# Two product-key expert layers on one core: softmax, transposes, small transfers and GpSimd's table emitted a slot or more after their input, and row gathers issued in every slot

## The chip, the cores and the metric

The kernel runs on one core of one Trainium2 chip. A core has TensorE (PE) for matrix products, with its weight loads shown apart (PEld), VectorE (DVE), ScalarE (ACT), GpSimd (POOL) and SyncE (SP), each with a queue of its own that it works off in order, and 16 DMA engines. The metric is the device time of one execution in microseconds (us).

## The reference, cut to what matters

Two blocks run one after the other on 256 tokens of width 1024. The first (four sequence mixers and an MLP) is not touched. The second adds 16 meta tokens (272 in all) and has two layers, each a mixer (pooling in layer 0, stick-breaking attention in layer 1) followed by a PEER layer: for every token 8 heads pick 16 of 16,384 experts each, and the token gets the sum of the picked experts' outputs.

```
s = einsum('bthpc,hpnc->bthpn', q, sub_keys)            # 8 heads, 2 halves, 128 sub-keys
top_s, top_i = lax.top_k(s, 16)                         # per half
cand_s = (top_s[..., 0, :, None] + top_s[..., 1, None, :])   # 256 candidates
cand_i = (top_i[..., 0, :, None] * 128 + top_i[..., 1, None, :])
best_s, best_pos = lax.top_k(cand_s, 16)
expert = take_along_axis(cand_i, best_pos)
gate = softmax(best_s)
act = gelu(einsum('btd,bthkd->bthk', hx, u[expert]))
y = einsum('bthk,bthkd->btd', gate * act, v[expert])
```

All of it is in fp32.

## The kernel before, in words

A PEER layer is `peer(l, ...)`, called for l = 0 and 1 (272 and 256 tokens). It does not gather the picked experts for most tokens. For 224 "dense" tokens it computes all 16,384 activations, multiplies them by a gate that is zero where the expert was not picked, and multiplies by all of v. The remaining 48 tokens (32 in layer 1) are "sparse": for each group of 16 of them 32 gathers bring the picked rows of u and then of v, one row in each of 128 partitions (512 KB per gather), and a DVE instruction, called a step here, multiplies or accumulates each.

Weights come in chunks of 128 x 1024 (512 KB). `_Stream` loads each into a raw buffer by SP's queue, ACT copies it rounded into a hi buffer (L256), and DVE or POOL subtracts the two into a lo buffer (L267; which one is said by `ULO` and `VLO`; in the U pass POOL takes the first 32 chunks and then three of each four). A projection (`proj`) is then 24 matmuls: 16 with hi and 8 with lo.

The **U pass** of a layer has 128 slots, `c` = 0 to 127, one u chunk in each. In the hand-made order of a slot come: `activate(c - 1)`, ACT's gelu of the chunk before (and, for tokens whose gates have already been made, DVE's product); `gates_out`, which takes finished gates out of PSUM; the hi and lo splits of a later chunk; sparse gathers and steps; ACT's `scaled` work for gates; DVE's routing work; the projection; gate matmuls. The first chunks do not need gates: a value waits in `row(c)` for them.

Routing work is the generator `routing()`: `route(8, ...)` for tokens 0 to 127 and then for the other dense and some of the sparse ones, in layer 0 also `topk_c` and `route(1, ...)` for the rest; then 56 groups of `onehots(j)`, one for each four dense tokens. A group's one-hot tiles oAB (compared with the index) and oHL (scaled by the gate, on DVE for every third group, on ACT for the others) feed 8 gate matmuls (`gates(j)`). There are three sets of these tiles. Each piece of routing says what it costs DVE, and a slot takes pieces until its budget `SLOT` is used up; yielding "slot" ends the slot's routing work, yielding a function runs it on PE after the slot's projection. When 128 slots are over and groups are left, the loop goes on with slots that have no projection.

Inside `route`: DVE adds the pairs of half scores (`pairs` after the change), POOL adds the pairs of indices into a table (L1006, L1009), `top16` finds the best 16 per head on DVE, ACT takes the exponent, DVE divides, PE transposes indices and gates to columns (`to_cols`). `finish_full(1)` sends the sparse tokens' indices and gates through DRAM by four small transfers on ACT's queue (L1069, L1070). Gathers (`fetch`, L1240) are issued on POOL's queue into two buffers in the U pass; `EARLY` says from which slot, `RS` how many steps a slot gets (0.4 and 0.2), and `held` are the buffers issued and not used.

The **V pass** has 128 chunks and two more gather buffers, `RV` steps per chunk. Most instructions carry line L200, the helper that records every operation.

Of the kernel before, what the change touches and what calls it, by code (L numbers as in the profile page):

```python
# [13 lines left out]
U32 = mybir.dt.uint32  # L14
# [5 lines left out]
P = 128  # L20
# [13 lines left out]
SLOT = 2800  # L34
# [254 lines left out]
def _build(nc, tc, A, O):  # L289
    pool_cm = tc.tile_pool(name="s", bufs=1)  # L290
    ps_cm = tc.tile_pool(name="ps", bufs=1, space=PSUM)
    with pool_cm as pool, ps_cm as pp:
# [604 lines left out]
        def peer(l, n, h, mixer, outer, qh, ql, end):  # L897
# [40 lines left out]
            best, pos, posf, ee, gg, dd, sm = (R(1) for _ in range(7))  # L938

# [27 lines left out]
            def top16(src, tv, iv):  # L967
                V.max(tv[0], src)
                V.max_index(iv[0].bitcast(U32), tv[0], src)
                V.match_replace(src, tv[0], src, -3.0e38)  # L970
                yield (600, 0, 0)
                V.max(tv[1], src)
                V.max_index(iv[1].bitcast(U32), tv[1], src)
                yield (400, 0, 0)
# [8 lines left out]
            def route(nh, tp, ix, finish):  # L983
# [12 lines left out]
                for eng, dst, s1, s2 in ((V, cand, v3(tp[:, 0]), v3(tp[:, 1])), (G, cex, v3(idxf[:, 0]), v3(idxf[:, 1]))):  # L996
# [14 lines left out]
                    yield ((1000, 0, 0) if eng is V else (0, 0, 1700))  # L1011
                for hd in range(nh):
                    yield from top16(cand[:, hd], halves(best[:, 0], 16 * hd), halves(pos[:, 0], 16 * hd))
                V.tensor_copy(posf[:, 0, 0:w], pos[:, 0, 0:w].bitcast(U32))
                V.tensor_sub(v3(dd[:, 0]), v3(best[:, 0]), v3(best[:, 0])[:, :, 0:1].broadcast_to([P, nh, 16]))
                S.activation(gg[:, 0, 0:w], dd[:, 0, 0:w], AF.Exp)
# [22 lines left out]
            def to_cols(e_src, g_src, a, b):  # L1039
# [6 lines left out]

                yield both
# [12 lines left out]
            def finish_full(j):  # L1060
                def g():
                    yield from to_cols(ee[:, 0, :], gg[:, 0, :], P * j, min(P * j + P, nd))
                    yield (1200, 0, 0)
                    if j:
                        a, m = nd - P, (SEQ - nd) // 16
                        pi = pos[:, 0].bitcast(U32)
                        V.tensor_copy(pi, ee[:, 0])
                        for dr, dst, src in ((sp_dr[0], sp_e, pi), (sp_dr[1], sp_g, gg[:, 0])):
                            nc.scalar.dma_start(dr[0:m].rearrange("g (t h) k -> (g t) (h k)", h=8), src[a:P])  # L1069
                            nc.scalar.dma_start(dst[:, 0:m], dr[0:m].rearrange("g p k -> p g k"))  # L1070
                        yield (150, 0, 0)
                return g
# [6 lines left out]
            def topk_c():  # L1079
                for hf in range(2):  # L1080
                    yield from top16(fold[:, hf], halves(topc[:, 0], 16 * hf), halves(idxc[:, 0], 16 * hf))
# [76 lines left out]
            scale_q, ready, mm, out_q = [], {}, [0], []  # L1158
# [84 lines left out]
            def gather():  # L1243
                q = mode["q"]
                if q == -1:
                    fetch(srow, sp_rows, row16[:, 0:1])
                elif q < len(js) and free:
                    g, j = js[q]
                    held.append(free.pop(0))
                    fetch(held[-1], A[f"ur{l}" if j < 16 else f"v{l}"], sp_e[:, g, j % 16:j % 16 + 1])  # L1250
                else:
                    return
# [16 lines left out]
            def sparse():  # L1269
                for i, (g, j) in enumerate(js):  # L1270
                    gather()
                    gather()
                    b, k = held.pop(0), j % 16
# [49 lines left out]
            with tc.manual_schedule():  # L1323
                c = 0
                while c < P or work is not None or scale_q or mm[0] < nq or out_q:
# [18 lines left out]
                    if c >= EARLY[l] and c >= mode["rdy"] and c < P:  # L1344
                        if c % 3 == 0 and mode["q"] < 4:
                            gather()
                        if mode["q"] > 0 and mode["n"] < 31:
                            bal_d -= 1300 * steps(RS[l])
# [25 lines left out]
                if c == P:  # L1374
                    activate(P - 1)

# [346 lines left out]
```

## Time and profile before

| | us |
|---|---|
| median of 3 runs (2188.49 to 2190.12) | 2190.11 |
| profiled execution, own time | 2184.81 |
| its span | 2182.8 |
| PE busy | 2062.6 (94%) |
| DVE busy | 1605.4 (74%) |
| ACT busy | 1271.5 (58%) |
| POOL busy | 1097.8 (50%) |
| mean granted TensorE clock | 0.966 of full speed |

In the span, layer 0's U pass runs from 418 to 862 us and its V pass from 870 to 1207; layer 1's from 1451 to 1844 and from 1852 to the end. Busy shares are means over stages; a stretch's own row says what holds it. A row of the timeline reads: start, duration, engine, line, operation, tiles out<-in, shapes, count, and in brackets how long the engine had stood idle before and what ended that.

### The profile page before, as it was taken

To read this page: it belongs to the slowest core of one execution; us is meant where nothing else is said; L and a number is where in the kernel's file an instruction comes from. 1 tells how busy PE (TensorE), PEld (TensorE's weight loads), DVE (VectorE), ACT (ScalarE), POOL (GpSimd) and SP (SyncE) were. 2 spreads that over 40 slices of the span, in tenths; PEclk is the share of its full clock that TensorE was granted. 3 is DMA by queue.
4 is the path that set the end of the run, shared out by engine and by line. 5 is a ranking of instruction groups with operands and counts; after the bars stand their busy time and mean duration, and the time that the engine had idled before them with its cause. 6 is when DMAs were issued, how large, how long until landed. Compare 5 with 4: busy or idle time off the path is not lost. (4 is left out here: it accounts for less than half of the span.)

```text
span 2182.8 us, 42173 instructions
## 1 busy us (share of the span) xinstructions
PE 2062.6 (94%) x15924; PEld 1981.2 (91%) x15924; DVE 1605.4 (74%) x3187; ACT 1271.5 (58%) x2572; POOL 1097.8 (50%) x671
## 2 busy tenths in 40 slices
PE   8889999888998888999999999988999999999999
PEld 6789998888998887999999988888999998999998
DVE  7964846998566567788887575699757766878875
ACT  4654444554876766555554665445688886555554
POOL 5746736576676656233332351457677766233210
PEclk8999999999999999999999997999999999999999
DMA  5336662354565656899997420534566667888874
GB/s 183 135 117 203 205 188 95 118 158 158 184 215 200 206 194 229 315 332 341 313 318 251 153 87 20 175 121 156 172 212 207 211 215 244 309 312 322 304 254 145
DMA packets 127964, 451.55 MB, mean 207 GB/s; under 512 B 16577, under 2 KB 19777, under 8 KB 126993
## 3 DMA queue, kind: packets, MB, share of 16 engines
q1 hardware_dynamic: 100192, 352.86, 49.0%
q0 software_dynamic: 24592, 88.32, 10.9%
q10 hardware_dynamic: 2976, 7.68, 1.0%
q8 instruction: 126, 2.06, 0.4%
q14 instruction: 78, 0.63, 0.1%
HBM read 445.00 MB, written 3.67 MB: 206 GB/s over the span
## 5 line engine op out<-in xcount | busy, mean ns | idle before, releaser
L200 PE MATMUL bank<-XX,hi 128*128 128x224 f32 (+3 forms) x7360 | 1152.9, 306 | 30.8 <-ACT hi L256 18.3
L200 PEld LDWEIGHTS bank<-XX,hi 128*128 128x128 f32 x7360 | 1017.9, 195 | 63.2 <-ACT hi L256 21.1
L267 POOL TENSOR_TENSOR lo<-raw,hi 128x1024 fp32r<-128x1024 f32 x276 | 674.6, 2456 | 448.8 <-ACT hi L256 398.9
L256 ACT ACTIVATE hi<-raw 128x1024 fp32r<-128x1024 f32 x616 | 650.2, 1057 | 410.3 <-PE bank L200 374.9
L200 PE MATMUL bank<-XX,lo 128*128 128x224 f32 (+2 forms) x4672 | 637.1, 278 | 20.8 <-POOL lo L267 14.2
L200 PEld LDWEIGHTS bank<-XX,lo 128*128 128x128 f32 x4672 | 601.4, 193 | 31.9 <-POOL lo L267 17.7
L267 DVE TENSOR_TENSOR lo<-raw,hi 128x1024 fp32r<-128x1024 f32 x340 | 434.5, 1278 | 168.0 <-ACT hi L256 143.7
L200 ACT ACTIVATE big<-bank 128x256 f32<-128x256 f32 (+45 forms) x400 | 126.3, 321 | 150.1 <-DVE big L200 95.8
L200 DVE TENSOR_TENSOR big<-big,bank 128x256 f32<-128x256 f32 (+41 forms) x313 | 94.4, 302 | 145.2 <-ACT big L200 135.8
L200 ACT ACTIVATE oHL<-oAB,picks 128x128 f16<-128x128 f16 x592 | 189.2, 391 | 19.1 <-DVE oAB L200 19.1
L200 DVE SCALAR_TENSOR_TENSOR big<-big 128x1024 f32<-128x1024 f32 (+5 forms) x89 | 109.2, 1232 | 42.1 <-DMA big<-ur,sp_e 32.3
L1240 POOL DMA_INDIRECT big<-ur,sp_e x56 | 80.3, 1434 | 89.2 <-DVE big L200 84.2
L1240 POOL DMA_INDIRECT big<-v,sp_e x47 | 70.6, 1501 | 107.9 <-DVE big L200 105.5
L200 DVE TENSOR_TENSOR oAB<-bank,picks 128x1024 f16<-128x1024 f32 (+1 forms) x112 | 114.0, 1035 | 0.0
L200 PE MATMUL bank<-big 128*128 128x128 f32 (+9 forms) x472 | 87.7, 314 | 11.6 <-ACT big L200 9.0
L200 ACT ACTIVATE XX<-big 128x224 fp32r<-128x224 f32 (+1 forms) x216 | 81.6, 378 | 28.4 <-DVE big L200 28.2
L200 ACT ACTIVATE big<-big 128x416 f32<-128x416 f32 (+5 forms) x120 | 53.9, 469 | 65.0 <-DVE big L200 58.8
L200 PE MATMUL bank<-oHL,oAB 128*128 128x128 f16 x896 | 68.7, 223 | 23.5 <-DVE oHL L200 13.9
L200 PEld LDWEIGHTS bank<-big 128*128 128x128 f32 (+3 forms) x472 | 66.8, 195 | 24.4 <-ACT big L200 11.3
L200 DVE TENSOR_TENSOR XX<-big,XX 128x224 fp32r<-128x224 f32 (+1 forms) x214 | 86.2, 404 | 0.0
L256 ACT ACTIVATE hi<-more 128x1024 fp32r<-128x1024 f32 x48 | 50.9, 1061 | 57.2 <-PE bank L200 55.2
L200 PEld LDWEIGHTS <-oAB 128*128 128x128 f16 x896 | 52.6, 99 | 27.5 <-issue 25.3
(189 smaller groups left out, 2389.7 us busy)
## 6 DMA issues: line engine op xcount, KB each, us to landing
raw<-u SPq DMA_DIRECT2D x256, 512.0 KB
raw<-v SPq DMA_DIRECT2D x208, 512.0 KB
raw<-w SPq DMA_DIRECT2D x64, 512.0 KB
more<-v SPq DMA_DIRECT2D x48, 512.0 KB
raw<-wq SPq DMA_DIRECT2D x32, 512.0 KB
raw<-win SPq DMA_DIRECT2D x16, 512.0 KB
raw<-wkv SPq DMA_DIRECT2D x16, 512.0 KB
raw<-wout SPq DMA_DIRECT2D x8, 512.0 KB
```

Of the source, the lines that this page charges most:

```text
L200: i = f(*a, **k)
L256: nc.scalar.activation(hi, raw, AF.Copy)
L267: eng.tensor_sub(self.lo[i % self.nh], raw, self.hi[i % self.nh].bitcast(F32))
L1240: nc.gpsimd.indirect_dma_start(out=dst, out_offset=None, in_=src, in_offset=bass.IndirectOffsetOnAxis(ap=at, axis=0))
```

## The change

It touches the order in which `peer` emits its work, and four numbers that the planner goes by. In `route`, POOL's table of index pairs is emitted with the fourth head's `top16` (or the last, where there are fewer) instead of right after DVE's pairs; a new "slot" stands ahead of ACT's exponent, and one ahead of the transposes. The planner's costs of `top16` go from 600 and 400 to 1000 and 550 in `route` and to 1150 and 750 in `topk_c`, and `SLOT` from 2800 to 2700. The sparse tokens' indices and gates are copied to rows of their own, and their transfers are put off: out two slots later, back five slots later. In the U pass a gather is issued in each slot in which a buffer is free, once those transfers are out, and a step is made only when the oldest gather is three slots old. In the V pass every free buffer is filled ahead of a step.

```
-SLOT = 2800
+SLOT = 2700
+            pout, gout = R(1)[:, 0], R(1)[:, 0]
-            def top16(src, tv, iv):
+            def top16(src, tv, iv, cost=(600, 400)):
-                yield (600, 0, 0)
+                yield (cost[0], 0, 0)
-                yield (400, 0, 0)
+                yield (cost[1], 0, 0)
-                for eng, dst, s1, s2 in ((V, cand, v3(tp[:, 0]), v3(tp[:, 1])), (G, cex, v3(idxf[:, 0]), v3(idxf[:, 1]))):
+                def pairs(eng, dst, s1, s2):
-                    yield ((1000, 0, 0) if eng is V else (0, 0, 1700))
+                pairs(V, cand, v3(tp[:, 0]), v3(tp[:, 1]))
+                yield (1000, 0, 0)
                 for hd in range(nh):
-                    yield from top16(cand[:, hd], halves(best[:, 0], 16 * hd), halves(pos[:, 0], 16 * hd))
+                    if hd == min(nh - 1, 3):
+                        pairs(G, cex, v3(idxf[:, 0]), v3(idxf[:, 1]))
+                    yield from top16(cand[:, hd], halves(best[:, 0], 16 * hd), halves(pos[:, 0], 16 * hd), (1000, 550))
+                yield "slot"
                 S.activation(gg[:, 0, 0:w], dd[:, 0, 0:w], AF.Exp)
                 yield "slot"
...
+                yield "slot"
                 yield both
...
-                        pi = pos[:, 0].bitcast(U32)
+                        pi = pout.bitcast(U32)
                         V.tensor_copy(pi, ee[:, 0])
-                        for dr, dst, src in ((sp_dr[0], sp_e, pi), (sp_dr[1], sp_g, gg[:, 0])):
-                            nc.scalar.dma_start(dr[0:m].rearrange("g (t h) k -> (g t) (h k)", h=8), src[a:P])
-                            nc.scalar.dma_start(dst[:, 0:m], dr[0:m].rearrange("g p k -> p g k"))
-                        yield (150, 0, 0)
+                        V.tensor_copy(gout, gg[:, 0])
+                        def there():
+                            for dr, src in ((sp_dr[0], pi), (sp_dr[1], gout)):
+                                nc.scalar.dma_start(dr[0:m].rearrange("g (t h) k -> (g t) (h k)", h=8), src[a:P])
+                        def back():
+                            for dr, dst in ((sp_dr[0], sp_e), (sp_dr[1], sp_g)):
+                                nc.scalar.dma_start(dst[:, 0:m], dr[0:m].rearrange("g p k -> p g k"))
+                        later.append((state["c"] + 2, there))
+                        later.append((state["c"] + 5, back))
+                        yield (300, 0, 0)
...
-                    yield from top16(fold[:, hf], halves(topc[:, 0], 16 * hf), halves(idxc[:, 0], 16 * hf))
+                    yield from top16(fold[:, hf], halves(topc[:, 0], 16 * hf), halves(idxc[:, 0], 16 * hf), (1150, 750))
...
-                    held.append(free.pop(0))
+                    held.append((free.pop(0), state["c"]))
...
-                    gather()
-                    gather()
-                    b, k = held.pop(0), j % 16
+                    while not held or (state["c"] >= P and free and mode["q"] < len(js)):
+                        gather()
+                    (b, _), k = held.pop(0), j % 16
...
-                    if c >= EARLY[l] and c >= mode["rdy"] and c < P:
-                        if c % 3 == 0 and mode["q"] < 4:
-                            gather()
-                        if mode["q"] > 0 and mode["n"] < 31:
-                            bal_d -= 1300 * steps(RS[l])
+                    while later and later[0][0] <= c:
+                        later.pop(0)[1]()
+                    if c >= EARLY[l] and c >= mode["rdy"] and c < P and not later:
+                        gather()
+                        mode["c"] = min(mode["c"] + RS[l], 1.5)
+                        if held and held[0][1] <= c - 3 and mode["n"] < 31:
+                            bal_d -= 1300 * steps(0)
...
+                state["c"] = P
+                mode["c"] = 0.0
```

The first place is POOL's queue at layer 0's first table, before and then after. `lo`, `raw` and `hi` are the buffers of u chunks; the rows of L1006 and L1009 (L1008 and L1011 in the changed kernel) are the table.

```order
L1101 DMA big<-big 16x2x128
L1006 TENSOR_TENSOR big<-big 128x8x16
L1006 TENSOR_TENSOR big<-big 128x8x8
L1006 TENSOR_TENSOR big<-big 128x8x5
L1006 TENSOR_TENSOR big<-big 128x8x4
L1006 TENSOR_TENSOR big<-big 128x8x3
L1009 TENSOR_TENSOR big<-big 128x8x2 x3
L1006 TENSOR_TENSOR big<-big 128x8x8
L267 TENSOR_TENSOR lo_76<-raw_72,hi_73 128x1024
L267 TENSOR_TENSOR lo_77<-raw_69,hi_74 128x1024
```

```order
L1118 DMA big<-big 16x2x128
L267 TENSOR_TENSOR lo_76<-raw_72,hi_73 128x1024
L267 TENSOR_TENSOR lo_77<-raw_69,hi_74 128x1024
L1008 TENSOR_TENSOR big<-big 128x8x16
L1008 TENSOR_TENSOR big<-big 128x8x8
L1008 TENSOR_TENSOR big<-big 128x8x5
L1008 TENSOR_TENSOR big<-big 128x8x4
L1008 TENSOR_TENSOR big<-big 128x8x3
L1011 TENSOR_TENSOR big<-big 128x8x2 x3
L1008 TENSOR_TENSOR big<-big 128x8x8
L267 TENSOR_TENSOR lo_78<-raw_70,hi_75 128x1024
```

The two lo splits that stood behind the table now stand ahead of it.

The second place is ACT's queue at layer 0's small transfers. The rows to `lo_4244<-bank` or `big<-bank` are gelus of whole chunks, `sp` is the DRAM buffer, `sp_e` and `sp_g` the sparse tokens' indices and gates.

```order
L256 ACTIVATE hi_73<-raw_71 128x1024
L1069 DMA sp<-big 32x128
L1070 DMA sp_e<-sp 128x2x16
L1069 DMA sp<-big 32x128
L1070 DMA sp_g<-sp 128x2x16
L200 ACTIVATE lo_4244<-bank_68 128x224
L256 ACTIVATE hi_74<-raw_72 128x1024
```

```order
L1080 DMA sp<-big 32x128 x2
L200 ACTIVATE big<-bank_62 128x224
L256 ACTIVATE hi_73<-raw_71 128x1024
L200 ACTIVATE big<-bank_68 128x224
L256 ACTIVATE hi_74<-raw_72 128x1024
L200 ACT_TABLE_LOAD
L200 ACTIVATE big<-big 128x16
L200 ACT_TABLE_LOAD
L200 ACTIVATE big<-bank_63 128x224
L256 ACTIVATE hi_75<-raw_69 128x1024
L1084 DMA sp_e<-sp 128x2x16
L1084 DMA sp_g<-sp 128x2x16
```

Both transfers out now go together, and those back stand three gelus and hi copies behind them, with the exponent of `route(1)` between.

The third place is ACT's queue at the end of layer 0's U pass. `bank<-bank` and `big<-bank` are the gelu of a chunk's gated and of its other tokens, `oHL` rows the scalings of a gate group (8 make one group), `WW` the first operands of the V pass.

```order
L200 ACTIVATE oHL_1_4252<-oAB_1_4249,picks 128x128 x4
L200 ACTIVATE bank_62<-bank_62 128x220
L200 ACTIVATE big<-bank_62 128x4
L256 ACTIVATE hi_73<-raw_70 128x1024
L200 ACTIVATE bank_68<-bank_68 128x220
L200 ACTIVATE big<-bank_68 128x4
L200 ACTIVATE WW_0_9402<-lo_4244 128x224
L200 ACTIVATE WW_1_9403<-lo_4244 128x224
```

```order
L200 ACTIVATE bank_68<-bank_68 128x188
L200 ACTIVATE big<-bank_68 128x36
L200 ACTIVATE oHL_2_4253<-oAB_2_4250,picks 128x128 x4
L200 ACTIVATE oHL_1_4252<-oAB_1_4249,picks 128x128 x8
L200 ACTIVATE oHL_2_4253<-oAB_2_4250,picks 128x128 x8
L200 ACTIVATE oHL_1_4252<-oAB_1_4249,picks 128x128 x8
L200 ACTIVATE oHL_2_4253<-oAB_2_4250,picks 128x128 x8
L200 ACTIVATE oHL_1_4252<-oAB_1_4249,picks 128x128 x8
L200 ACTIVATE WW_0_9375<-lo_4244 128x224
L200 ACTIVATE WW_1_9376<-lo_4244 128x224
```

When the last chunk's gelu runs, 188 tokens have their gates instead of 220, and the scalings of five groups and a half stand between it and the V pass.

## Rows read from the trace of the kernel before

**Rows 1.** Busy time by stretch: stretch, its length, then each engine's busy us.

```profile
core 0: us, PE busy (x) PEld busy (x) DVE busy (x) ACT busy (x) POOL busy (x), PEclk, DMA share, GB/s
418.40:541.20 122.80, 104.22 (x866) 102.43 (x865) 108.87 (x354) 56.12 (x87) 85.82 (x62) 0.94 0.48 153
...
618.50:861.80 243.30, 211.15 (x1896) 205.13 (x1897) 162.86 (x268) 164.16 (x452) 155.32 (x78) 0.96 0.61 200
...
869.80:1207.00 337.20, 335.42 (x2133) 319.73 (x2133) 274.51 (x382) 176.16 (x269) 110.68 (x70) 0.99 0.88 309
1451.30:1558.20 106.90, 93.75 (x768) 92.66 (x766) 97.60 (x333) 45.77 (x71) 73.37 (x47) 0.92 0.47 150
1558.20:1844.20 286.00, 285.09 (x2746) 283.70 (x2746) 195.32 (x353) 239.30 (x642) 204.29 (x91) 1.00 0.63 209
```

**Rows 2.** Timeline of PE, two projections' starts in layer 1's late U pass.

```profile
1710.34 1.95 PE L200 MATMUL bank<-XX,hi 128*128 128x224 f32 x16
...
1713.02 1.95 PE L200 MATMUL bank<-XX,hi 128*128 128x224 f32 x16
```

**Rows 3.** Work on the tiles oHL by stretch: PE (gate matmuls), DVE, ACT.

```profile
618.50:861.80 243.30, 26.26 (x312) 15.82 (x13) 67.56 (x212) 0.96 0.61 200
...
1558.20:1844.20 286.00, 31.18 (x440) 21.92 (x18) 94.52 (x296) 1.00 0.63 209
```

**Rows 4.** Waits of PE, 1558.2 to 1844.2: us, times, longest.

```profile
PE bank L200 <- POOL lo L267: 0.8, 2, 0.4
```

**Rows 5.** Timeline of POOL at the first table of layer 0, then of layer 1.

```profile
426.47 1.77 POOL L1006 TENSOR_TENSOR big<-big 128x128 f32<-128x128 f32 x5 [3.75 <-DVE big L200]
...
429.03 6.99 POOL L267 TENSOR_TENSOR lo<-raw,hi 128x1024 fp32r<-128x1024 f32 x3
...
1461.81 1.86 POOL L1006 TENSOR_TENSOR big<-big 128x128 f32<-128x128 f32 x5 [7.52 <-DVE big L200]
```

**Rows 6.** Timeline of ACT: layer 0's second exponent, layer 1 after the small transfers.

```profile
483.26 0.31 ACT L200 ACTIVATE big<-big 128x128 f32<-128x128 f32 x1 [6.11 <-DVE big L200]
...
1556.88 0.36 ACT L200 ACTIVATE lo<-bank 128x224 f32<-128x224 f32 x1 [9.57 <-DMA sp<-big]
```

**Rows 7.** Waits of DVE, 618.5 to 861.8: us, times, longest.

```profile
DVE big L200 <- DMA big<-ur,sp_e: 27.2, 7, 6.6
DVE big L200 <- DMA big<-v,sp_e: 16.4, 4, 5.7
```

**Rows 8.** DVE's instructions by form, 600 to 861: busy us, mean ns.

```profile
L200 DVE TENSOR_TENSOR oAB<-bank,picks 128x1024 f16<-128x1024 f32 x28 | 34.0, 1215 | 0.0
L200 DVE SCALAR_TENSOR_TENSOR big<-big 128x1024 f32<-128x1024 f32 x16 | 29.8, 1861 | 32.3 <-DMA big<-ur,sp_e 32.3
...
L200 DVE TENSOR_TENSOR oAB<-bank,picks 128x512 f16<-128x512 f32 x14 | 9.5, 681 | 0.0
```

**Rows 9.** Timeline of DVE, the last group's product out of PSUM.

```profile
868.63 0.28 DVE L200 TENSOR_TENSOR lo<-lo,bank 128x128 f32<-128x128 f32 x1
868.83 0.55 DVE L200 TENSOR_TENSOR big<-big,bank 128x384 f32<-128x384 f32 x1
```

**Rows 10.** Timeline of PE, from the last projection to the V pass, both layers.

```profile
863.63 1.06 PE L200 MATMUL bank<-XX,lo 128*128 128x224 f32 x8
...
869.82 3.35 PE L200 MATMUL bank<-WW,hi 128*128 128x448 f32 x8 [3.78 <-DVE WW L200]
...
1846.01 1.05 PE L200 MATMUL bank<-XX,lo 128*128 128x224 f32 x8
1851.59 3.25 PE L200 MATMUL bank<-WW,hi 128*128 128x448 f32 x8 [4.53 <-DVE big L200]
```

**Rows 11.** ACT's scalings by form, 618.5 to 861.8: busy us, mean ns.

```profile
L200 ACT ACTIVATE oHL<-oAB,picks 128x128 f16<-128x128 f16 x212 | 67.8, 391 | 19.1 <-DVE oAB L200 19.1
```

**Rows 12.** Timeline of DVE, one sparse step in layer 0.

```profile
715.97 1.22 DVE L200 SCALAR_TENSOR_TENSOR big<-big 128x1024 f32<-128x1024 f32 x1
```

**Rows 13.** The page's groups: POOL's lo splits of the whole span.

```profile
L267 POOL TENSOR_TENSOR lo<-raw,hi 128x1024 fp32r<-128x1024 f32 x276 | 674.6, 2456 | 448.8 <-ACT hi L256 398.9
```

**Rows 14.** Waits of POOL's gathers, 618.5 to 861.8: us, times, longest.

```profile
POOL big L1240 <- DVE big L200: 4.2, 2, 2.9
```

More of the change, by code (lines that the diff above doesn't have):

```diff
@@ L1157, in peer @@
             nq = nd // 4
-            scale_q, ready, mm, out_q = [], {}, [0], []
+            scale_q, ready, mm, out_q, later = [], {}, [0], [], []
             def routing():
@@ L1248, in gather @@
                     g, j = js[q]
-                    held.append(free.pop(0))
-                    fetch(held[-1], A[f"ur{l}" if j < 16 else f"v{l}"], sp_e[:, g, j % 16:j % 16 + 1])
+                    held.append((free.pop(0), state["c"]))
+                    fetch(held[-1][0], A[f"ur{l}" if j < 16 else f"v{l}"], sp_e[:, g, j % 16:j % 16 + 1])
                 else:
```

## The prediction

> **What bounds the kernel now.** I read the stretches first: the two layers' U passes, cut where TensorE (PE) starts slots 0, 35 and 61 of layer 0 and slots 0 and 31 of layer 1 and where it starts the last one, beside a V pass [rows 1]. The V pass is PE's: 335.4 of 337.2 us busy, so nothing that only reorders work gains there. In the U passes PE is busy for 211 of 243 us in layer 0's sparse stretch, 104 of 123 and 94 of 107 us in the two routing stretches, but 285 of 286 us in layer 1's late one. That last one is the yardstick. A slot without gates is 2.68 us from one projection to the next [rows 2]. Layer 1's late stretch has 96 slots and 440 gate matmuls, 55 groups of 8 [rows 3], and PE waits there for 0.8 us in all [rows 4]: a group costs (286.0 - 96 x 2.68) / 55 = 0.52 us. By this price the stretches should have taken:
> - layer 0, slots 0 to 34, one group: 35 x 2.68 + 0.5 = 94.3; it took 122.8, so 28.5 is lost (two sets of transposes included).
> - layer 0, slots 61 to 126, 39 groups: 66 x 2.68 + 39 x 0.52 = 197.2; it took 243.3, so 46.1 is lost.
> - layer 1, slots 0 to 30, one group: 83.6; it took 106.9, so 23.3 is lost.
> Together 97.9 us. This counts the time after a stall too, when PE runs at a lower granted clock (0.94, 0.96 and 0.92 as means of these stretches, 1.00 in the yardstick).
>
> Then who makes PE wait. In routing, GpSimd's (POOL's) first table waits for VectorE's (DVE's) indices, 3.75 us in layer 0 and 7.52 in layer 1, with the lo splits of three u chunks queued behind it [rows 5]. ScalarE (ACT) stands at the softmax exponent for 6.11 us, and in layer 1 it stands 9.57 us because four small transfers share its queue and each second one needs the first landed [rows 6]. Behind both are ACT's gelus and hi copies that PE needs next. In the sparse stretch DVE waits for gathered rows: 27.2 us for u rows and 16.4 for v rows, 43.6 in eleven waits [rows 7], about the 46.1 that PE loses. Alternate gathers are issued only two slots ahead of their step there; in layer 1, where a gather has five slots, no such wait is among the yardstick's 286 us.
>
> **The change, part by part.** *Table, exponent, transposes, small transfers.* No instruction is removed; each moves behind work that was queued after it. The table goes behind two more lo splits, the exponent and the transposes a slot on, the transfers out two slots on and those back five, so that ACT no longer stands for a landing. The route's work also gets a larger price in the planner and slots a smaller budget, so that DVE is asked for less per slot. What is late next: DVE begins layer 1's routing later behind PE than layer 0's (its table waited twice as long [rows 5]), and two splits are about 5 us, short of the 7.5. Left over, as estimates: layer 0 4.5 us (transposes 1.6, start 3), layer 1 7 (the same transposes, 2.5 at table and exponent, 3 at the lower clock behind them). Gain 28.5 + 23.3 - 11.5 = 40.3. Bounds: 0 and 48. The new copy on DVE is one short instruction per layer, beside other work.
>
> *Gathers.* Each slot may now issue one when a buffer is free, and a step takes its row three slots or more later; in the order of layer 0 that is four slots mostly, in layer 1 nine. The number of steps in the U passes stays at 30 and 16. In layer 0 two more slots are 6 us; the eleven waits' longest were 6.6 and 5.7, their mean 4.0 [rows 7]. So most go, and I leave 5 us of the 46.1: gain 41.1. Bounds: 23 (the first rival) and 46. In the V pass more buffers in flight gain nothing, since PE is the bound.
>
> *The tail, the price.* The larger costs delay the gate work: the first group runs in slot 45 instead of 34 in layer 0, and in slot 40 instead of 30 in layer 1. Groups left when u chunks run out: layer 0 nine of 56 instead of one, layer 1 four instead of none. These run with no projections beside them, so that DVE sets their pace. In layer 0 that is one gelu product of 0.3, then three groups with both halves on DVE at 0.68 + 0.68 + 1.21 = 2.57, five comparisons at 1.21 [rows 8], and nine products out of PSUM at 0.28 + 0.55 = 0.83 [rows 9]: 0.3 + 7.7 + 6.1 + 7.5 = 21.6; with the last group's matmuls and the split of the first V operand some 2 us more, 23.6 from the last projection to the V pass. Before, that is 864.69 to 869.82, 5.1 us [rows 10]. So +18.5, less eight groups that left the slots, 8 x 0.52 = 4.2: +14.3. ACT's share, five groups of eight scalings at 67.8 / 212 = 0.32 us [rows 11], is 12.8 and lies beside it. Layer 1 likewise: four groups come to 12.7, before 1847.06 to 1851.59, 4.5 [rows 10]: +8.2, less 2.1: +6.1. Together +20.4. Bounds: +15, if the last groups overlap better with what is queued; +29, if they run one after the other in part (comparison, scalings, matmuls, product: 1.2 + 2.5 + 0.5 + 0.8 = 5.0 us a group at worst). I take the sum by DVE, since three sets of tiles let the next group start early. The V pass starts at the lower clock before too (3.35 and 3.25 us for its first eight matmuls [rows 10]), so that isn't charged again.
>
> Sum: -40.3 - 41.1 + 20.4 = -61.0 against the profiled execution's own 2184.81 (span 2182.8): 2123.8. The median of the runs shown, 2190.11, is 5.3 above it; on that scale **2129**.
>
> **The rivals.** *DVE becomes the bound in layer 0's sparse stretch.* A step there took 1.86 us in the mean [rows 8] and 1.22 where nothing stood beside it [rows 12]. DVE's 162.9 busy us over 66 slots are 2.47 of the 2.99 that a clean slot takes. With 0.4 steps a slot it would fill the slot once a step takes 1.86 + 0.52 / 0.4 = 3.2 us; at 3.85, 0.27 us in each of 66 slots, 18 us more than forecast: half of the 46.1 stays, and the time is 2147. For it: the means show that a step's length isn't its own. Against it: layer 1's stretch has steps and splits beside each other and no stall.
> The Trainium skill, page "SBUF — State Buffer", section "Who interferes with whom", says that a DVE instruction with two inputs in SBUF and a GpSimd instruction that reads SBUF exclude each other for the whole instruction, so denser steps beside lo splits would cost more than the steps alone. With a POOL split at 2.46 us [rows 13], by this rule at worst each step waits for one whole split, 1.22 + 2.46 = 3.68 us, and the stretch would take 66 x 0.4 x (3.68 - 3.2) = 13 us more, 2142 by this estimate; the rows agree in part, since 1.86 is a quarter of such a wait above 1.22.
>
> *The route's stalls only move.* If DVE stays behind by more than the added slots, ACT and POOL wait at their new places for as long: 40.3 us come back, 2169. For it: 7.52 us at layer 1's table. Against it: the waits are at most 10 us and each place got a slot (2.7) to five.
>
> *Slower: gathers hold POOL.* A gather now stands in POOL's queue as soon as the plan counts a buffer free, though DVE may still read it; lo splits stand behind it, and PE behind these. There are some 46 gathers in the two U passes. It decides from 61 / 46 = 1.3 us lost per gather; before, such a wait was met twice, 4.2 us in all [rows 14]; at their mean of 2.1 each it is 46 x 2.1 = 97, and 2226. Against it: POOL is idle for 88 of the sparse stretch's 243 us [rows 1], and three lo buffers stand between it and PE.
>
> *Nothing changes* (within 0.2%, 4.4 us, which is about what a measurement of this kernel can tell from no change): if the stalls have another cause than the waits named, as DVE's total work, their sum stays and the tail is eaten by small gains: 2190.
>
> **How the numbers follow.** Forecast 0.68 (own range 2111 to 2143), DVE-bound 0.13, moved stalls 0.08, gathers hold POOL 0.07, nothing 0.04. Low end: no leftover but the transposes (-13) and a tail of +15 (-5): 2110. High end: the DVE-bound time with a tail of +29: 2155. Left out: the moved stalls, the slower case, the last one. Faster 0.68 + 0.13 + 0.08 = 0.89, same 0.04, slower 0.07.
>
> **What would show it.** Right: slots 61 to 126 of layer 0 in some 200 us, with fewer groups, and no DVE wait for a gather above 2 us; routing stretches at some 2.8 us a slot and no ACT wait over 3 us at the exponent or at a transfer; 23 and 13 us between the last projection and the V pass; V passes unchanged. Wrong: DVE over 95% busy in the sparse stretch (first rival); ACT or POOL waits of 5 us and more in routing (second); POOL waiting for DVE at gathers (third); a tail at 5 us a group.

## The result and the profile after

The changed kernel takes 2130.39 us (median of four runs, 2128.17 to 2136.01) against 2189.3 for the kernel before (four runs, 2177.73 to 2190.12). The ratio is put at 0.9761, 95% interval 0.9738 to 0.9783; the two medians by themselves give 0.9731. The gain is 52 us by the one and 59 by the other. The forecast was 2129. The profiled executions took 2129.01 and 2184.81, 55.8 us apart.

These are the stretches of the changed kernel, cut at the same slots as in [rows 1], with the two tails (from the start of slot 127 to the V pass) between. The columns are stretch, length, busy us of each engine with instruction counts, then the granted clock of TensorE (PE), the DMA share and GB/s.

```profile
core 0: us, PE busy (x) PEld busy (x) DVE busy (x) ACT busy (x) POOL busy (x), PEclk, DMA share, GB/s
418.30:517.20 98.90, 96.31 (x856) 95.53 (x855) 90.41 (x286) 51.89 (x79) 83.62 (x53) 1.00 0.56 183
593.20:802.10 208.90, 200.51 (x1899) 196.63 (x1898) 168.74 (x263) 160.34 (x440) 157.44 (x78) 1.00 0.71 237
802.10:829.90 27.80, 18.33 (x100) 10.26 (x97) 25.66 (x44) 18.03 (x58) 2.79 (x3) 0.58 0.34 112
829.90:1165.00 335.10, 333.26 (x2134) 317.82 (x2134) 273.83 (x382) 176.48 (x270) 110.65 (x71) 0.99 0.86 307
1405.80:1494.20 88.40, 85.44 (x759) 84.61 (x758) 82.31 (x300) 46.89 (x72) 75.46 (x48) 1.00 0.54 178
1494.20:1776.80 282.60, 282.11 (x2708) 281.14 (x2707) 196.08 (x358) 227.97 (x595) 199.56 (x92) 1.00 0.64 214
1776.80:1794.45 17.65, 11.11 (x75) 6.95 (x74) 14.77 (x28) 12.14 (x40) 1.92 (x3) 0.68 0.48 160
```

PE is granted the full clock in every stretch of the U passes now, where it was 0.92 to 0.96 in three of them; the two tails are new places at 0.58 and 0.68. Set beside the forecast, in us:

| stretch | before | after | difference | forecast |
|---|---|---|---|---|
| layer 0, slots 0 to 34 | 122.8 | 98.8 | -24.0 | -24.0 |
| layer 0, slots 35 to 60 | 77.3 | 76.1 | -1.2 | -3.6 (seven groups fewer) |
| layer 0, slots 61 to 126 | 243.3 | 208.9 | -34.4 | -41.1 |
| layer 0, last projection to V pass | 5.1 | 24.9 | +19.8 | +18.5 |
| layer 1, slots 0 to 30 | 106.9 | 88.3 | -18.6 | -16.3 |
| layer 1, slots 31 to 126 | 286.0 | 282.7 | -3.3 | -2.1 (groups) |
| layer 1, last projection to V pass | 4.5 | 14.8 | +10.3 | +8.2 |
| all the rest | | | -4.4 | 0 |

The last line is the V passes, the attention and what lies ahead, mostly the stretch from layer 0's V pass to layer 1's slot 0, 581.5 before and 575.9 after. In the runs below, most of which leave the order there untouched, that stretch takes 575.6 to 583.4; nothing is read into it. Slots 0 to 34, by contrast, take 98.7 to 98.8 us in every run below that leaves table, new slots and prices as changed.

The waits that were to go went. This is POOL at the first tables of layer 0 and layer 1 (timeline: start, duration, instruction, then the idle time before it and what ended it), which answer [rows 5]:

```profile
428.33 1.33 POOL L1008 TENSOR_TENSOR big<-big 128x128 f32<-128x128 f32 x5 [0.30 <-DVE big L200]
...
1416.28 1.79 POOL L1008 TENSOR_TENSOR big<-big 128x128 f32<-128x128 f32 x5 [0.93 <-DVE big L200]
```

3.75 and 7.52 us have become 0.30 and 0.93. Each layer's U pass has two long exponents. The 6.11 us of [rows 6] are the shorter stand of layer 0 before the change (layer 1's second is the same); at the first of each layer ACT stood for longer:

```profile
438.97 0.31 ACT L200 ACTIVATE big<-big 128x128 f32<-128x128 f32 x1 [9.42 <-DVE big L200]
...
1474.17 0.31 ACT L200 ACTIVATE big<-big 128x128 f32<-128x128 f32 x1 [11.79 <-DVE big L200]
```

After the change the four stands are 2.9 and 3.6 us in layer 0, 3.1 and 3.9 in layer 1; three are still over the 3 us that the prediction gave as a sign:

```profile
441.33 0.31 ACT L200 ACTIVATE big<-big 128x128 f32<-128x128 f32 x1 [2.94 <-DVE big L200]
...
491.95 0.31 ACT L200 ACTIVATE big<-big 128x128 f32<-128x128 f32 x1 [3.62 <-DVE big L200]
...
1428.81 0.31 ACT L200 ACTIVATE big<-big 128x128 f32<-128x128 f32 x1 [3.05 <-DVE big L200]
...
1479.67 0.31 ACT L200 ACTIVATE big<-big 128x128 f32<-128x128 f32 x1 [3.88 <-DVE big L200]
```

And DVE's waits for gathers in layer 0's slots 61 to 126 (total, times, longest), 43.6 us in [rows 7]:

```profile
DVE big L200 <- DMA big<-ur,sp_e: 4.9, 3, 2.0
```

### The profile page after: what moved, and what is told of

It reads as the page before. It is cut to its first block, busy times and chain, and to the rows that moved or that the text cites. A ratio compares the mean times of both kernels' runs of the same rounds, so it can differ in the third digit from the quotient of the medians.

```text
span 2127.0 us, 42088 instructions
## 1 busy us (share of the span) xinstructions
PE 2048.0 (96%) x15922; PEld 1960.2 (92%) x15924; DVE 1619.5 (76%) x3169; ACT 1264.3 (59%) x2541; POOL 1095.2 (51%) x671
## 4 chain that ended last, share of the span: by engine, by line
PE 69%; DVE 13%; issue 4%; ACT 4%; POOL 3%; DMA 1%; POOLq 0%; ACTq 0%; DVEq 0%
PE bank L200 69%; DVE big L200 9%; POOL lo L267 2%; ACT hi L256 1%; ACT oHL L200 1%; DVE bank L200 1%; DVE lo L267 1%; DVE XX L200 1%; DVE oAB L200 1%; POOL big L1257 1%; ACT big L200 1%; DMA big<-ur,sp_e 0%; DMA raw<-u 0%; DVE lo L200 0%; POOL big L943 0%
## 5 line engine op out<-in xcount | busy, mean ns | idle before, releaser
L200 PE MATMUL bank<-XX,hi 128*128 128x224 f32 (+3 forms) x7360 | 1135.0, 303 | 21.4 <-ACT hi L256 9.3
L200 PEld LDWEIGHTS bank<-XX,hi 128*128 128x128 f32 x7360 | 1001.5, 192 | 52.7 <-ACT hi L256 12.0
L200 PE MATMUL bank<-XX,lo 128*128 128x224 f32 (+2 forms) x4672 | 630.0, 276 | 7.2 <-POOL lo L267 5.7
L200 PEld LDWEIGHTS bank<-XX,lo 128*128 128x128 f32 x4672 | 595.0, 192 | 17.3 <-POOL lo L267 8.2
L200 ACT ACTIVATE big<-bank 128x256 f32<-128x256 f32 (+33 forms) x391 | 125.1, 325 | 152.0 <-DVE big L200 79.6
L200 DVE TENSOR_TENSOR big<-big,bank 128x256 f32<-128x256 f32 (+38 forms) x295 | 91.8, 312 | 122.1 <-ACT big L200 112.1
L200 DVE SCALAR_TENSOR_TENSOR big<-big 128x1024 f32<-128x1024 f32 (+5 forms) x89 | 117.2, 1321 | 17.9 <-DMA big<-ur,sp_e 9.1
L200 PE MATMUL bank<-oHL,oAB 128*128 128x128 f16 x896 | 79.5, 226 | 15.0 <-ACT oHL L200 11.2
```

Of the source, the lines that this page charges most:

```text
L200: i = f(*a, **k)
```

## The experiments

Stretch lengths below are from PE's slot starts in each run's profile; "loss" is length less 2.68 us per slot and 0.52 per gate group, the price that the prediction made from [rows 2 to 4].

**The two halves apart.** First the gather part alone on the kernel before (prices, slots, table and transfers as there):

```
+                    while not held or (state["c"] >= P and free and mode["q"] < len(js)):
+                        gather()
...
+                        gather()
+                        mode["c"] = min(mode["c"] + RS[l], 1.5)
+                        if held and held[0][1] <= c - 3 and mode["n"] < 31:
+                            bal_d -= 1300 * steps(0)
```

> The kernel before with the gather part of the change alone (a gather in every slot with a free buffer, steps three slots or more later, all free buffers filled in the V pass); routing, its prices and the small transfers as before. Theory: the parts add up, so the sparse stretch of layer 0 falls from 243 us to some 209, DVE's waits for gathers from 43.6 to about 5 us, the routing stretches stay at 123 and 107 us, the tails at 5 us; time 2189 - 35 - 3 = 2151. Rival: the sparse stretch was cured by the smaller budgets and later gates, not by the longer lead; then it stays above 230 us and the time above 2175.

It took 2143.31 us (before, 2186.91 beside it; ratio 0.9796, 0.9770 to 0.9822). Slots 61 to 126 of layer 0, DVE's steps there (by form: busy us, mean ns, idle before), and the first two routing stretches:

```profile
418.20:540.70 122.50, 104.67 (x864) 103.44 (x864) 109.00 (x354) 55.66 (x86) 84.62 (x62) 0.93 0.46 152
619.00:821.20 202.20, 199.00 (x1899) 196.33 (x1899) 166.07 (x271) 161.51 (x445) 158.62 (x78) 1.00 0.72 244
1408.10:1515.20 107.10, 92.48 (x767) 91.39 (x767) 97.71 (x333) 45.91 (x71) 73.36 (x48) 0.94 0.45 150
```

```profile
L200 DVE SCALAR_TENSOR_TENSOR big<-big 128x1024 f32<-128x1024 f32 x13 | 24.1, 1856 | 0.0
L200 DVE SCALAR_TENSOR_TENSOR big<-big,sp_w 128x1024 f32<-128x1024 f32 x12 | 18.6, 1552 | 0.0
```

No step waits for a gather (0.0 idle), the stretch fell from 243.3 to 202.2, and the routing stretches stayed. The longer lead alone cured the sparse stretch; the rival is out. It did so by 7 us more than with the routing part beside it (208.9).

Then the routing part alone: the changed kernel with the gather lines as before.

> The changed kernel with its gather part undone: the routing part alone. Theory: routing stretches as in the changed kernel (99 and 88 us), tails 25 and 15 us, and the sparse stretch of layer 0 back at about 243 us with 40 us and more of DVE waits for gathers; time 2130 + 37 = 2167, which with the gathers alone adds up to the whole change. Rival: the parts lean on each other, and this one alone gives less than 10 us (2180 or more) or more than 40.

It took 2161.2 us (ratio 0.9871, 0.9846 to 0.9897). Routing stretches 98.7 and 88.3, tails 22.7 and 13.9, and slots 61 to 126 at 238.4 with DVE waiting 35.2 us for gathers, somewhat less than the 40 expected:

```profile
DVE big L200 <- DMA big<-ur,sp_e: 19.9, 8, 6.0
DVE big L200 <- DMA big<-v,sp_e: 15.3, 6, 6.4
```

The halves gave 43.6 and 25.7 us apart and some 57 together (2186.91 less the 2130.39 of another session), so about 12 do not add up. That has a place: in slots 61 to 126 the gathers bring 243.3 - 202.2 = 41.1 us alone and 238.4 - 208.9 = 29.5 beside the routing part, 11.6 less.

**What is still lost in the sparse stretch.** The changed kernel loses 11.7 us there, with no gather wait above 2.0 us and DVE 81% busy. Its steps have grown; by form, in slots 61 to 126:

```profile
L200 DVE SCALAR_TENSOR_TENSOR big<-big 128x1024 f32<-128x1024 f32 x14 | 36.2, 2586 | 4.9 <-DMA big<-ur,sp_e 4.9
...
L200 DVE SCALAR_TENSOR_TENSOR big<-big,sp_w 128x1024 f32<-128x1024 f32 x12 | 19.8, 1652 | 0.0
```

A u-row step takes 2.59 us in the mean, 1.86 before [rows 8], 1.22 alone [rows 12]. The longest, on DVE's and POOL's timelines:

```profile
630.01 5.67 DVE L200 SCALAR_TENSOR_TENSOR big<-big 128x1024 f32<-128x1024 f32 x1
```

```profile
628.89 0.95 POOL L1257 DMA_INDIRECT big<-ur,sp_e  x1
629.86 4.72 POOL L267 TENSOR_TENSOR lo<-raw,hi 128x1024 fp32r<-128x1024 f32 x2
```

Two lo splits begin on POOL 0.15 us ahead of the step and end at 634.58; the step ends 1.1 us later, about what it takes by itself. Of the 29 such steps of that U pass the nine with no split beside them take 1.22 to 1.28 us, the twenty others 1.2 to 5.7. So fewer steps there:

```
-RS = (0.4, 0.2)
+RS = (0.2, 0.2)
-RV = (0.53, 0.47)
+RV = (0.65, 0.47)
```

> The changed kernel with 0.2 steps per slot instead of 0.4 in layer 0's U pass and 0.65 instead of 0.53 in its V pass, which takes the steps that are left. In layer 0's slots 61 to 126 the changed kernel still loses 11.7 us against clean slots. Theory: the loss comes of steps that stand still while POOL splits a u chunk beside them, so half the steps bring it to 6 us or less, the V pass, where no split is on POOL, takes its further steps at 1.22 to 1.28 us each without a loss; time 2124. Rival: the loss is made by gates and ACT's copies there, and stays: 2130; or DVE's added work in the V pass shows, and the time is above 2132.

It took 2118.93 us (ratio 0.9686, 0.9664 to 0.9709). Slots 61 to 126 of layer 0:

```profile
591.00:788.30 197.30, 196.90 (x1898) 195.68 (x1898) 140.35 (x248) 162.30 (x440) 140.38 (x64) 1.00 0.63 211
```

39 gate groups as before and PE idle for 0.4 us: the loss is gone, more than halved, at the same gate work and nearly the same ACT time (162.3 for 160.3). The V pass bore its fourteen further steps without a loss. One thing more went with them: only fifteen u-row steps are left in this U pass, so ACT's gelu of a group's sixteen sparse products, which has to wait for the sixteenth, falls into the V pass. What that wait cost is told below; this run alone does not part it from the meeting with splits.

To see the two engines' meeting by itself, every fourth lo split of the V passes, where all were DVE's, went to POOL:

```
+VLO = ("V" * 8 + "GVVV" * 30,) * 2
```

> The changed kernel with every fourth lo split of both V passes (from chunk 8 on) on POOL instead of DVE. In the changed kernel no split is on POOL in a V pass, and all 49 + 38 sparse steps there take 1.22 to 1.28 us. Theory: DVE's step and POOL's split exclude each other, so a step that meets a split lasts longer by the time both stand side by side, up to 1.25 + 2.46 = 3.7 us, while steps that meet none stay at 1.22 to 1.28; the time stays within 10 us, since PE is the bound there. Rival: the long steps of the U pass come of the gathers and other traffic beside them, of which the V pass has more; then all V pass steps stay at 1.28 us.

It took 2132.7 us (one run). The steps stayed at 1.22 to 1.28 us, as the rival had it: theory's forecast for them failed, since each starts ahead of the split in its slot. What waited was the next instruction in DVE's queue, the subtraction that makes a V pass operand's low part. Its rows by form in the changed kernel and in this one (835 to 1160 us), and one meeting on the timelines of DVE and POOL:

```profile
L200 DVE TENSOR_TENSOR XX<-big,XX 128x224 fp32r<-128x224 f32 x96 | 37.0, 385 | 0.0
```

```profile
L200 DVE TENSOR_TENSOR XX<-big,XX 128x224 fp32r<-128x224 f32 x96 | 79.8, 832 | 11.2 <-ACT XX L200 10.9
```

```profile
881.19 2.58 DVE L200 TENSOR_TENSOR XX<-lo,XX 128x224 fp32r<-128x224 f32 x1
```

```profile
880.86 2.66 POOL L267 TENSOR_TENSOR lo<-raw,hi 128x1024 fp32r<-128x1024 f32 x1 [1.67 <-ACT hi L256]
```

0.385 us has become 0.832 in the mean: of the 96, the 73 with no split beside them take 0.37 to 0.39, the 23 that met one 2.27 in the mean. The one shown, the same subtraction on another operand (`XX<-lo,XX`), takes 2.58 and ends 0.25 us after the split. So it is the split that holds DVE, and not the step's kind: both kinds of instruction shown here as held have two inputs in SBUF. It is not the gathers: in the changed kernel's U pass three steps had a gather's issue beside them and no split, and took 1.27 to 1.28. And DVE's comparisons, with one input in PSUM (`bank`), keep the length of [rows 8] in the changed kernel's slots 61 to 126, though most of them run beside a split:

```profile
L200 DVE TENSOR_TENSOR oAB<-bank,picks 128x1024 f16<-128x1024 f32 x25 | 30.4, 1215 | 0.0
```

That is what the Trainium skill, page "SBUF — State Buffer", section "Who interferes with whom", says: such a DVE instruction and a GpSimd instruction that reads SBUF do not go side by side, and one that comes second waits until the first has ended. The trace agrees: 1.22 us alone, 5.67 behind two splits. Which of them goes first is not settled by their order alone there: the second split began 2.2 us after the step and still went ahead of it.

**The routing part, one edit undone at a time** (single runs, read by their stretches). The table right behind DVE's pairs again:

```
-                    if hd == min(nh - 1, 3):
+                    if hd == 0:
```

> The changed kernel with GpSimd's table emitted right behind DVE's pairs again; all else as changed (routing stretches 98.8 and 88.3 us). Theory: POOL again waits for DVE's indices at the first table, 3 to 4 us in layer 0 and about 7 in layer 1, lo splits behind it; layer 0 loses 4 us, layer 1 some 9 with the lower clock behind it; 2143. Rival: with the later exponent DVE comes early enough and the three lo buffers cover the rest: less than 3 us in all.

2140.79 us. The routing stretches took 100.8 and 91.8, +2.0 and +3.5; the table waits as it did, 3.75 us in layer 0 and 7.21 in layer 1,

```profile
1424.04 1.77 POOL L1008 TENSOR_TENSOR big<-big 128x128 f32<-128x128 f32 x5 [7.21 <-DVE big L200]
```

and PE feels about half of it: between theory and rival. The rest of this run's 10 us lies in the sparse stretch (212.4) and in the one from layer 0's V pass to layer 1 (579.7), which this edit does not touch.

Without the two new slots:

```
-                yield "slot"
                 S.activation(gg[:, 0, 0:w], dd[:, 0, 0:w], AF.Exp)
...
-                yield "slot"
                 yield both
```

> The changed kernel without the two new slots (ahead of the exponent and ahead of the transposes). Theory: ACT stands at each exponent again, 6 to 9 us, four of them over the two layers, each costing PE 4 us and the lower clock behind it: routing stretches +10 us each; gate work starts five slots earlier and three groups fewer are left in each layer, -6 and -6 in the tails; 2138. Rival: the higher prices alone keep ACT's wait under 3 us, then only the tails show: 2120.

2138.92 us. Routing stretches 107.5 and 96.1, +8.7 and +7.8; ACT stands at the exponents for 5.2 to 5.9 us, short of the 6 to 9 expected; tails 16.2 and 10.8, -8.7 and -3.9. The time is theory's. Of the 16.5 us that the new slots gain in the routing stretches, they pay 12.6 back in the tails.

The small transfers in a row again:

```
-                        later.append((state["c"] + 2, there))
-                        later.append((state["c"] + 5, back))
+                        for dr, dst, src in ((sp_dr[0], sp_e, pi), (sp_dr[1], sp_g, gout)):
+                            nc.scalar.dma_start(dr[0:m].rearrange("g (t h) k -> (g t) (h k)", h=8), src[a:P])
+                            nc.scalar.dma_start(dst[:, 0:m], dr[0:m].rearrange("g p k -> p g k"))
```

> The changed kernel with the four small transfers issued in a row again, each back right behind its out. Theory: ACT stands for two landings, about 9 us per layer, of which PE feels 5 to 6 and the lower clock behind it; both lie behind slot 30: 2130 + 2 x 7 = 2144. Rival: ACT is ahead of PE there by enough to hide it: under 3 us in all.

2141.22 us. ACT stands behind the transfers for 7.4 us in layer 0 and 8.4 in layer 1:

```profile
1529.65 0.36 ACT L200 ACTIVATE big<-bank 128x224 f32<-128x224 f32 x1 [8.40 <-DMA sp<-big]
```

The stretch in which they fall grew by 4.5 us in layer 0 (76.1 to 80.6) and 4.2 in layer 1 (87.7 to 91.9), less than the seven expected, and well above the rival's. The run's other 2 us lie elsewhere.

Last the planner's prices and the budget as before:

```
-SLOT = 2700
+SLOT = 2800
-... halves(pos[:, 0], 16 * hd), (1000, 550))
+... halves(pos[:, 0], 16 * hd))
-... halves(idxc[:, 0], 16 * hf), (1150, 750))
+... halves(idxc[:, 0], 16 * hf))
```

> The changed kernel with the planner's prices of the top 16 search at 600 and 400 and the slot budget at 2800 again; the new slots, the table and the transfers as changed. Gate work then starts in slot 39 instead of 44 in layer 0 and three groups are left there instead of nine, none in layer 1. Theory: DVE, 91% busy in the routing stretch, falls behind the plan, and the exponent and the table wait for it again, though less than before: routing stretches +8 us each, tails -13 and -9: about 2124. Rival: the prices are what cures the stalls, and the stretches go back to 115 us and more: 2140.

2144.93 us. Routing stretches 111.0 and 101.3, +12.2 and +13.0; tails 6.5 and 5.1, -18.4 and -9.6. In layer 1's routing stretch ACT waits for DVE at the two exponents:

```profile
ACT big L200 <- DVE big L200: 18.5, 2, 9.3
```

That is 9.2 to 9.3 us at each, with the new slots in place, where 5.2 to 5.9 stood without the slots: prices and budget together matter more than the slots. Which of the two does it was not tried. Neither theory (+8) nor rival (115 and more) had the size; of the four edits undone, this is the largest part of the routing's gain and of the tail's cost at once, and in layer 0 it costs as much as it brings.

**The tail.** A budget of 3000 once routing is over, so that no group is left:

```
+                    slot = SLOT if c < mode["rdy"] else 3000
+                    bal_d, bal_a = min(bal_d, 0) + slot, min(bal_a, 0) + slot
```

> The changed kernel with a slot budget of 3000 instead of 2700 once the routing work is over (eight slots after it), so that no gate group is left behind the last slot in either layer. Theory: the tails go from 24.9 and 14.8 us back to about 5, the gate matmuls that then stand in slots cost 0.52 us a group (nine and six groups): -20 + 4.7 and -10 + 2: time 2107. Rival: DVE can't do more per slot, PE waits for it in the slots and the tail's time comes back there: 2120 to 2135.

2132.47 us, no gain (ratio 0.9741, 0.9716 to 0.9765). Tails 5.2 and 2.5, but slots 61 to 126 took 220.9 and 213.1 (208.9 and 195.0 in the changed kernel):

```profile
1582.20:1795.30 213.10, 205.81 (x1925) 200.61 (x1923) 151.57 (x267) 167.87 (x461) 140.56 (x66) 0.99 0.61 204
```

```profile
DVE big L200 <- ACT big L200: 48.0, 40, 2.9
...
ACT big L200 <- DVE big L200: 30.9, 37, 2.1
```

The rival's size, but its reason isn't shown: neither engine is full (71 and 79%), and DVE and ACT wait for each other just as long in the changed kernel's same slots (1581.8 to 1776.8), where PE waits for nothing:

```profile
DVE big L200 <- ACT big L200: 50.0, 39, 2.5
ACT big L200 <- DVE big L200: 26.6, 32, 1.9
```

What is new is on PE: it stands 4.1 us for POOL's lo splits and 2.0 for ACT's scalings, and the matmuls of 42 groups take 28.2 us where those of 37 took 21.1, as they do when they have to wait for scalings one by one. That points to ACT. So ACT's part was cut instead: on the run with 0.2 steps, every second group's scalings go to DVE instead of every third's.

```
-                if j % 3:
+                if j % 2:
```

> The run with 0.2 steps per slot in layer 0's U pass and 0.65 in its V pass (2119 us), with every second gate group scaled on DVE instead of every third, which takes ACT's scalings of some nine groups away in each layer and puts as many 2 x 0.68 + 1.21 - 1.21 = 1.36 us on DVE. Four groups instead of nine are then left in layer 0 and none in layer 1. Theory: ACT's budget is what holds the gates back (81% busy in layer 1's late stretch, DVE 69%), so the tails fall from 23 and 15 us to some 12 and 4, the slots take 0.52 us more per group, 15 + 5 and 11 + 4 groups apart: -22 + 6: 2103. Rival: DVE falls behind in the slots, as with the larger budget, and PE waits there: 2115 to 2125.

2104.12 us (ratio 0.9623, 0.9598 to 0.9648), as theory had it: tails 12.0 and 5.6, slots 61 to 126 at 196.5 in both layers with PE never idle:

```profile
598.30:794.80 196.50, 196.50 (x1915) 196.00 (x1913) 153.96 (x275) 155.09 (x406) 139.15 (x63) 1.00 0.64 213
1565.20:1761.70 196.50, 196.50 (x1915) 195.99 (x1913) 152.26 (x272) 152.92 (x404) 139.16 (x64) 1.00 0.63 212
```

From there, a budget of 2800 once routing is over (the edit above with 2800):

> The run with every second gate group scaled on DVE (2104 us), with a slot budget of 2800 instead of 2700 once routing is over: no gate group is then left in either layer. Theory: DVE is 78% and ACT 79% busy in layer 0's late stretch, so the slots bear the four groups more: tail of layer 0 from 12 to some 5 us, slots +2 us: 2099. Rival: as with the budget of 3000, DVE and ACT then wait for each other in the slots and PE for them: 2104 or more.

and, instead of it, 0.1 steps:

```
-RS = (0.2, 0.2)
+RS = (0.1, 0.1)
-RV = (0.65, 0.47)
+RV = (0.72, 0.54)
```

> The run with every second gate group scaled on DVE (2104 us), with 0.1 steps per slot in both U passes (0.2 there) and 0.72 and 0.54 in the V passes (0.65 and 0.47). No gate group is left in either layer, at the unchanged budget of 2700. Theory: fewer steps meet POOL's splits, DVE has room for the gates, the V passes' DVE (some 90% busy then) still keeps up: tail of layer 0 12 to 5 us, slots +2: 2099. Rival: the V passes' steps come too thick, PE waits for DVE there, or the last steps stand behind the end of the V pass: 2104 or more.

2099.08 and 2102.91 us, with ratios 0.9626 (0.9602 to 0.9649) and 0.9633 (0.9601 to 0.9664). Layer 0's tail fell to 5.9 and 6.8 us, about as expected, and slots 61 to 126 rose by 2.7 and 4.9 (three groups more). By their ratios to the kernel before, measured beside each, the last three cannot be told apart; all are faster than both kernels.

## Why the prediction was right

*The bound and the price of a clean slot.* Right. With the waits gone layer 1's late stretch and the 0.2-step run take what 2.68 and 0.52 us give, within 1.1.

*Table, exponent, transposes, transfers: gain 40.3.* It was 24.0 + 18.6 = 42.6. The waits at table and exponent shrank as described, and among ACT's waits there is none for a landing any more. The rival that they only move had a grain of truth: 2.9 to 3.9 us still stand at exponents, too short for PE to wait more than 1.5 for a hi copy at once. What the working passed over are the longer stands at the first exponents (9.42 and 11.79), and the weight of prices and budget: undone by themselves they cost 12 to 13 us of each routing stretch, the two slots 8 to 9, the table 2 to 3.5. These overlap, since they come to more than the gain in layer 1.

*Gathers: gain 41.1.* The wait went (43.6 to 4.9), but the gain was 34.4 there, with 39 groups as before, where the prediction had fewer: this is the term that was mis-sized, the 5 us left being 11.7. The rival's mechanism, steps held by POOL's splits, was at work at about a third of its size. The mean u-row step grew to 2.59 us, short of the 3.2 from which that rival was to decide; PE lost 11.7 all the same, 8.4 of it standing still. Nor was the longest step the dearest: 0.96 us of PE's standing follow the one of 5.67, none that of 4.07. PE's longest stand comes of a step of 2.98:

```profile
698.18 2.98 DVE L200 SCALAR_TENSOR_TENSOR big<-big 128x1024 f32<-128x1024 f32 x1 [1.21 <-DMA big<-ur,sp_e]
...
701.20 0.22 ACT L200 ACTIVATE sp_w<-sp_w 128x16 f32<-128x16 f32 x1 [3.58 <-DVE big L200]
...
705.15 2.04 PE L200 MATMUL bank<-XX,hi 128*128 128x224 f32 x16 [2.23 <-ACT hi L256]
```

It is a group's sixteenth step; ACT's gelu of the sixteen products waits for it, with hi copies behind it in the queue, and PE waits for those. The working measured the step by its mean and left out what stands behind its result in another queue. With the routing part out the same gathers left 5.0, and that gelu did not wait; there and here the loss depends on where steps fall against splits. How they come to meet more often beside the routing part wasn't tried apart.

*The tail: +20.4.* It came to 19.8 + 10.3 - (1.2 + 3.3 of the other stretches) = 25.6. In layer 0 nine groups were left, as counted. In layer 1 it was six, not four: the gate matmuls up to slot 126 are 400 of 448, and two of the six groups run right behind the last projection. DVE's sum was nearly right for layer 0 (24.9 for 23.6), and short by 2 in layer 1 (14.8 for 12.7). What it left out stands in DVE's queue between the last projection and the groups: a step and a lo split of the V pass in layer 0, two lo splits in layer 1.

```profile
805.51 1.28 DVE L200 SCALAR_TENSOR_TENSOR big<-big,sp_w 128x1024 f32<-128x1024 f32 x1
806.86 1.23 DVE L267 TENSOR_TENSOR lo<-raw,hi 128x1024 fp32r<-128x1024 f32 x1
...
1779.70 1.23 DVE L267 TENSOR_TENSOR lo<-raw,hi 128x1024 fp32r<-128x1024 f32 x1
...
1781.68 1.22 DVE L267 TENSOR_TENSOR lo<-raw,hi 128x1024 fp32r<-128x1024 f32 x1 [0.47 <-ACT hi L256]
```

DVE starts on the groups' work 3.7 us after the last projection in layer 0 and 3.9 us after it in layer 1, where the sum has 0.3. That layer 0 came out so near is luck: its groups took 2 us less than the sum, since on DVE's timeline an instruction's row starts about 0.1 us before the one ahead of it ends. On PE the tails look like this, layer 0 first; the last row is ACT's, beside layer 0's last group:

```profile
803.95 1.06 PE L200 MATMUL bank<-XX,lo 128*128 128x224 f32 x8
...
826.39 2.31 PE L200 MATMUL bank<-oHL,oAB 128*128 128x128 f16 x8 [1.10 <-ACT oHL L200]
829.92 3.36 PE L200 MATMUL bank<-WW,hi 128*128 128x448 f32 x8 [1.22 <-DVE WW L200]
...
1779.53 1.44 PE L200 MATMUL bank<-oHL,oAB 128*128 128x128 f16 x16
```

```profile
825.94 2.44 ACT L200 ACTIVATE oHL<-oAB,picks 128x128 f16<-128x128 f16 x8 [1.81 <-DVE oAB L200]
```

The last group's eight matmuls take 2.31 us where eight take 0.62 in slots. The reason is not the granted clock, though that fell to a mean of 0.58 in this tail, where PE stands idle between groups: each matmul starts when the next of ACT's eight scalings, 2.44 us in all, has ended. The estimate of some 2 us for the last group and the first operand held.

So +6.7 in the gathers and +5.2 in the tail were too little charged, -2.3 in routing and -4.4 elsewhere too much: 5.2 short of the 61.0 forecast. The slower rival, gathers holding POOL, did not come: POOL waits for DVE at gathers four times in that stretch, 1.4 us at most. That the median of 2130.39 is within 1.4 of 2129 is luck: the terms miss the profiled execution by 5.2, and the 5.3 added for the scale of the medians was 1.4 in the changed kernel.

## What to carry to other kernels

An in-order queue that stands for another engine's result costs all that is queued behind it, so put such an instruction behind work whose input is already there, and price the producer honestly: prices and budget together did more here than any one of the moves. Then ask what the saved time no longer covers: each microsecond taken out of the slots left gate work over, and a third of the gain went to two tails in which PE stands between gate groups. Balance engines by moving work between them (ACT's scalings to DVE, steps to a pass with room) rather than by promising more per slot.

## What the runs showed of the hardware

A DVE instruction with two inputs in SBUF and a POOL subtraction of 128 x 1024 do not run side by side here: 1.22 us became 5.67 behind two splits, and 0.38 became 2.58 behind one. It goes the other way too: the split beside that one took 2.66 us, where most take 2.40; a step of 1.21 had begun 0.8 us ahead of it. The long duration is written on the DVE instruction's own row, as busy time and not as a wait. DVE's busy share of 81% in the sparse stretch thus holds about 24 us of standing still: 36.2 + 19.8 us for 14 and 12 steps that alone would take 17 and 15.
